# Turning q and k of the differential heads on VectorE instead of TensorE, and making the weights' parts for two row tiles at once

## The chip, the cores and the metric

The kernel runs on one core of a Trainium2 chip. Its time is the device time of one execution in microseconds (us). A core has these engines: PE (TensorE, the matrix unit; the loading of its stationary operand is shown as PEld), DVE (VectorE), ACT (ScalarE), POOL (GpSimd) and SP (SyncE, which here issues DMAs). Each works through a queue of its own, in order; semaphores hold an instruction until what it needs is there.

## The reference

Two layers, each on x of 256 rows (the sequence) and 2048 columns, all float32. A layer normalises x by rows (RMSNorm), multiplies by one wide weight `w_in` (2048 x 7168), and deals the columns out to three groups:

- a short gated convolution (768 columns wide): y_A = B * conv3(C * x_A) * silu(g_A);
- differential attention, 6 heads of 128 columns. q and k of a head are two halves of 64, each RMS-normalised by itself. The scores of each half go through a softmax with a distance bias, and the head's output is the first half's weighted v minus lambda times the second's, normalised and gated by silu(g_D);
- cross attention into 256 memory rows, 4 heads of 128; the memory has a projection of its own, `w_mem_kv`.

The three results side by side (2048 columns) are multiplied by `w_out` and added to x.

```
q = rmsnorm(d_q.reshape(b, s, 6, 2, 64), diff_q_norm_g[l])
k = rmsnorm(d_k.reshape(b, s, 6, 2, 64), diff_k_norm_g[l])
sc = einsum('bhcqd,bhckd->bhcqk', q, k) * 64**-0.5 + bias
o = softmax(sc) @ v ;  o[:, :, 0] - lam * o[:, :, 1]
```

## The kernel before, in words

**Three products for one.** Weights and the stationary side are split into a high part (rounded to the type float32r, on which PE runs fast) and a low part (the rest). A product is high x high + high x low + low x high: three matmuls, lines 237 to 239. A weight is streamed 128 rows (one *row tile*) x 512 columns at a time against two stationary tiles (the 256 rows of x are two tiles of 128), so one row tile of weights is used by six matmuls.

**Making the parts.** `load_w` (L204) loads two row tiles (a *pair*, 512 KB, CK = 2) by one DMA on SP's queue into `raw` (4 buffers), and then, for each row tile by itself, ACT writes `hi` (L218) and DVE writes `lo` = raw - hi (L219). For `w_mem_kv` a gain is multiplied in at the same time (L221, L222). `hi` and `lo` have 8 buffers each (PARTS), one for a row tile.

**Blocks.** `block` (L228) computes 512 output columns into two accumulators `acc` in PSUM: it goes through the 16 row tiles of the weight, a pair at a time. After each pair it takes one step of *side work* from a queue (`run_side`, L168): generators that transpose, split and score what earlier blocks left. `flush_side` empties the queue.

**The stages.** The memory's keys and values of both layers come first (4 blocks), then for each layer: six blocks for q, k, v and gate of the differential heads (L591, b = 0 to 5), two for the memory heads, six for the convolution, and four for the output projection (L690). The blocks b = 0, 1, 2 hold q and k: b = 0 has q of heads 0 to 3, b = 1 the rest of q and k of heads 0 and 1, b = 2 k of heads 2 to 5.

**q and k.** After each of these blocks `normed` (L296) takes the sums of squares by halves (ACT L302, DVE L303), an rsqrt by a chain of small DVE instructions (L159 to L163), and writes the scaled block `nat`, one 128x512 tile for each 128 rows (DVE L311). `qk_T` (L388) then turns it: for each of the two tiles, four 128x128 transposes on PE into a PSUM tile `ptq` (L394), and from there ACT and DVE write the split parts into `yT`: for q a high copy (ACT L402) and a low (DVE L403); for k two high copies with the gain (ACT L412, L413), a low (DVE L417) and a copy of it to the other 64 partitions (DVE L419). Both tiles are two steps of side work.

**Heads.** `diff_head` (L424) has the score matmuls L429 and L430, which read those parts, then bias, maximum, softmax (L434 to L447), transposes and the product with v (`weighted`, L356). They are put into the side queue after b = 5.

**Square turns.** `turn32` (L332) is there before the change for the gate of the convolution: DVE's transpose works on squares of 32x32, and 16 instructions, each for one pair of 32-partition groups, turn a whole 128x128 pattern; four of them are one step of side work.

**What sets the order.** The text of the program gives priorities; a scheduler that plans with estimated durations puts the instructions of each engine into their final order when the program is built, and buffers are handed out in that order. On the chip each engine keeps that order. So a change in one helper can move instructions of others.

Of the kernel before, what the change touches and what calls it, by code (L numbers as in the profile page):

```python
# [18 lines left out]
P = 128  # L19
D_MODEL = 2048  # L20
SEQ = 256
DEPTH = 2
NT = SEQ // P
# [4 lines left out]
CG = W_CONV // P  # L28
DH = W_DIFF // P
HALF = 64  # L30
MH = W_MEM // P
EPS = 1e-6
NB = 512
CK = 2
PARTS = 8
# [8 lines left out]
def encoder(ctx: ExitStack, tc: tile.TileContext, x, mem, norm_g, w_in, conv_w, conv_b,  # L44
            dq_g, dk_g, lq1, lk1, lq2, lk2, head_g, mem_norm_g, w_mem_kv, mq_g, mk_g, w_out, out):
    nc = tc.nc
# [8 lines left out]
    wp = pool("wp", 3)  # L55
    keep = pool("keep", 1)
    tmp = pool("tmp", 2)
# [3 lines left out]
    ps_t = pool("ps_t", 2, PSUM)  # L61
# [66 lines left out]
    kgain = const.tile([P, DEPTH], F32, name="kgain")  # L128
# [37 lines left out]
    side = deque()  # L166
# [21 lines left out]
    def in_order(*ins):  # L188

        if pinned[0]:  # L190
            for i in ins:
                tc.keep_in_program_order(i)
# [11 lines left out]
    def load_w(rows, cols, gains_of=None, step=CK, head=False):  # L204

        raw = wp.tile([P, CK, NB], F32, tag="raw", name=nm("raw"), bufs=4)
        at = 0
        for lo, n in cols:
            for j in range(0, CK, step):
                (nc.scalar if head and j == 0 else nc.sync).dma_start(  # L210
                    raw[:, j:j + step, at:at + n], rows[j * P:(j + step) * P, lo:lo + n].rearrange("(j p) c -> p j c", p=P))
            at += n
        parts = []
        for j in range(CK):
            hi = wp.tile([P, NB], F32R, tag="hi", name=nm("hi"), bufs=PARTS)
            lo_ = wp.tile([P, NB], F32R, tag="lo", name=nm("lo"), bufs=PARTS)
            if gains_of is None:
                nc.scalar.copy(hi, raw[:, j])  # L218
                nc.vector.tensor_tensor(lo_, raw[:, j], hi.bitcast(F32), ALU.subtract)  # L219
            else:  # L220
                ins = [nc.scalar.activation(hi, raw[:, j], AF.Copy, scale=gains_of(j)),  # L221
                       nc.vector.scalar_tensor_tensor(lo_, raw[:, j], gains_of(j), hi.bitcast(F32),  # L222
                                                      ALU.mult, ALU.subtract)]
                in_order(*ins)
            parts.append((hi, lo_))
        return parts

    def block(stat, w, cols, order, steps=1, gain=None, before=None, apart=0):  # L228

# [63 lines left out]
    def col(st, which, t):  # L293
        return st[:, which, t:t + 1]

    def normed(acc, gs, st):  # L296

        ng = NB // gs
        ss = small.tile([P, NT, ng], F32, tag=f"ss{ng}", name=nm("ss"))
        for t in range(NT):  # L300
            sq = tmp.tile([P, NB], F32, tag="nat", name=nm("sq"), bufs=4)
            nc.scalar.activation(sq, acc[t], AF.Square)  # L302
            nc.vector.tensor_reduce(ss[:, t], sq.rearrange("p (g d) -> p g d", d=gs), AX.X, ALU.add)  # L303
            nc.vector.tensor_scalar(ss[:, t], ss[:, t], col(st, R2_64 if gs == HALF else R2_128, t), EPS,
                                    ALU.mult, ALU.add)
        r = rsqrt(ss.rearrange("p t g -> p (t g)"), NT * ng).rearrange("p (t g) -> p t g", t=NT)
        res = []
        for t in range(NT):
            nc.vector.tensor_scalar(r[:, t], r[:, t], col(st, R, t), None, ALU.mult)
            y = tmp.tile([P, NB], F32, tag="nat", name=nm("nat"), bufs=4)  # L310
            nc.vector.tensor_tensor(y.rearrange("p (g d) -> p g d", d=gs),  # L311
                                    acc[t].rearrange("p (g d) -> p g d", d=gs),
                                    r[:, t].unsqueeze(2).to_broadcast([P, ng, gs]), ALU.mult)
            res.append(y)
        return res

    def turn(nat, dests):

# [13 lines left out]
    def turn32(dst, src):  # L332

        n = src.shape[-1] // P
        B = 32
        for b in range(P // B):
            for a in range(P // B):
                nc.vector.transpose(
                    dst[b * B:(b + 1) * B, 0:n].rearrange("p j (t a c) -> p t j a c", a=P // B, c=B)[:, :, :, a, :],
                    src[a * B:(a + 1) * B].rearrange("p t (j b c) -> p t j b c", b=P // B, c=B)[:, :, :, b, :])  # L340
            yield
# [43 lines left out]

    ROWS = (slice(0, HALF), slice(HALF, P))

    def qk_T(l, yT, k2, nat, q, k):  # L388

        for t in range(NT):  # L390
            ts = slice(t * P, (t + 1) * P)
            pt = ps_t.tile([P, 4, P], F32, tag="t", name=nm("ptq"))
            for j in range(4):
                nc.tensor.transpose(pt[:, j, :], nat[t][:, j * P:(j + 1) * P], ident)  # L394
            if q is not None:
                c0, h0, nh = q
                a = c0 // P
                for c in range(2):
                    own, other = ROWS[c], ROWS[1 - c]
                    src = pt[own, a:a + nh, :]  # L400
                    hi = yT[own, c, h0:h0 + nh, ts]
                    nc.scalar.copy(hi, src)  # L402
                    nc.vector.tensor_tensor(yT[other, c, h0:h0 + nh, ts], src, hi.bitcast(F32), ALU.subtract)  # L403
            if k is not None:
                c0, h0, nh = k
                a = c0 // P
                for c in range(2):
                    own, other = ROWS[c], ROWS[1 - c]
                    src = pt[own, a:a + nh, :]
                    g = kgain[own, l:l + 1]  # L410
                    hi = yT[own, c, CG + h0:CG + h0 + nh, ts]
                    nc.scalar.activation(hi, src, AF.Copy, scale=g)  # L412
                    nc.scalar.activation(yT[other, c, CG + h0:CG + h0 + nh, ts], src, AF.Copy, scale=g)  # L413
                    for at, n, dst, d0 in ((0, min(nh, 4 - h0), yT, CG + DH + h0), (4 - h0, h0 + nh - 4, k2, 0)):
                        if n > 0:
                            lo = dst[own, c, d0:d0 + n, ts]
                            nc.vector.scalar_tensor_tensor(lo, pt[own, a + at:a + at + n, :], g,  # L417
                                                           hi[:, at:at + n].bitcast(F32), ALU.mult, ALU.subtract)
                            nc.vector.tensor_copy(dst[other, c, d0:d0 + n, ts], lo)  # L419
            yield  # L420

    scored = set()

# [140 lines left out]
    for l in range(DEPTH):  # L564
# [10 lines left out]
        acc = block(memT, w_mem_kv[l], [(W_MEM, NB)], ALLK, gain=gm, before=mem_square if l == 0 else None)  # L575
# [7 lines left out]
    for l in range(DEPTH):  # L583
        st = stats_of(ssx, "st")


        yT = T_tile("yT")
        k2 = keep.tile([P, 2, DH - 4, SEQ], F32R, tag="bgT", name=nm("k2"))
        v = keep.tile([P, NT, W_DIFF], F32, tag="v", name=nm("v"))
        ga = keep.tile([P, NT, W_DIFF], F32, tag="ga", name=nm("ga"))  # L590
        for b in range(6):  # L591
            acc = block(xT, w_in[l], [(C_D + b * NB, NB)], ALLK)
            if b < 3:
                side.append(qk_T(l, yT, k2, normed(acc, HALF, st),
                                 (0, 0, 4) if b == 0 else (0, 4, 2) if b == 1 else None,
                                 (256, 0, 2) if b == 1 else (0, 2, 4) if b == 2 else None))
            else:
                for t in range(NT):
                    if b == 3:
                        nc.scalar.activation(v[:, t, 0:NB], acc[t], AF.Copy, scale=col(st, R, t))  # L600
                    elif b == 4:
                        nc.scalar.activation(v[:, t, NB:768], acc[t][:, 0:256], AF.Copy, scale=col(st, R, t))
                        silu2(ga[:, t, 0:256], acc[t][:, 256:512], st, t)
                    else:
                        silu2(ga[:, t, 256:768], acc[t], st, t)
# [66 lines left out]
        acc = block(xT, w_in[l], [(C_X + NB, 256), (C_C + NB, 256)], ALLK)  # L672
# [5 lines left out]
        acc = block(xT, w_in[l], [(C_C, NB)], ALLK)  # L678
# [57 lines left out]
```

## Time and profile before

| | |
|---|---|
| median of 3 runs | 960.23 us (959.88 to 960.38) |
| the profiled execution | 960.4 us, of which the span of the program's instructions is 958.6 us |
| PE busy | 99%, 4458 matmuls |
| DVE busy | 72%, 1560 instructions |
| ACT busy | 55%, 1091 instructions |
| granted clock of PE | 1.00 |
| DMA | 175.27 MB, mean 183 GB/s |

The page of the profile gives busy times by engine and by group of instructions (a line of the kernel, an engine, an operation, the tiles written and read). A group's row ends with its busy time, the mean ns of one instruction, and the idle time of the engine just before them with what ended it. Two instructions of one engine can overlap: a matmul lasts longer than the distance to the next. The waits list who waited for whom: total us, times, longest. The timeline lists instructions by start and duration; "x2" is a row of two that follow each other.

### The profile page before, as it was taken

To read this page: it belongs to the slowest core of one execution; us is meant where nothing else is said; L and a number is where in the kernel's file an instruction comes from. 1 tells how busy PE (TensorE), PEld (TensorE's weight loads), DVE (VectorE), ACT (ScalarE), POOL (GpSimd) and SP (SyncE) were. 2 spreads that over 40 slices of the span, in tenths; PEclk is the share of its full clock that TensorE was granted. 3 is DMA by queue.
4 is the path that set the end of the run, shared out by engine and by line. 5 is a ranking of instruction groups with operands and counts; after the bars stand their busy time and mean duration, and the time that the engine had idled before them with its cause. 6 is when DMAs were issued, how large, how long until landed. Compare 5 with 4: busy or idle time off the path is not lost.

```text
span 958.6 us, 13432 instructions
## 1 busy us (share of the span) xinstructions
PE 952.0 (99%) x4458; PEld 788.6 (82%) x4458; DVE 691.9 (72%) x1560; ACT 555.4 (58%) x1091; POOL 1.4 (0%) x8
## 2 busy tenths in 40 slices
PE   9999999999999999999999999999999999999998
PEld 6888888888888888888888888888888888888886
DVE  5767778865787888576766678856787788577663
ACT  5857756755656655554555556754666655554442
POOL 0000000000000000000000000000000000000000
PEclk9999999999999999999999999999999999999999
DMA  7775565576554554655555666566455555554661
GB/s 251 266 272 188 178 179 178 172 215 187 171 174 154 164 159 150 208 176 175 176 178 193 181 179 190 177 202 197 153 174 176 157 171 172 172 182 161 218 221 66
DMA packets 103530, 175.27 MB, mean 183 GB/s; under 512 B 6318, under 2 KB 29732, under 8 KB 103460
## 3 DMA queue, kind: packets, MB, share of 16 engines
q1 hardware_dynamic: 102116, 173.09, 57.3%
q10 hardware_dynamic: 1344, 1.33, 0.5%
q8 instruction: 35, 0.57, 0.2%
q14 instruction: 35, 0.29, 0.1%
HBM read 172.29 MB, written 2.10 MB: 182 GB/s over the span
## 4 chain that ended last, share of the span: by engine, by line
PE 94%; DMA 2%; DVE 2%; ACT 1%; issue 1%; ACTq 0%; DVEq 0%
PE acc L237 29%; PE acc L239 29%; PE acc L238 29%; DMA raw<-in_w_mem_kv_dram 2%; PE po L368 2%; DVE lo L222 1%; PE ptT L361 1%; ACT hi L221 1%; PE pt L506 1%; PE s L476 1%; PE s L430 1%; PE s L429 1%; PE ptq L394 1%; PE py L353 0%; PE pt L323 0%
## 5 line engine op out<-in xcount | busy, mean ns | idle before, releaser
L218 ACT CAST hi<-raw 128x512 fp32r<-128x512 f32 x576 | 355.2, 621 | 323.4 <-PE acc L239 199.2
L219 DVE TENSOR_TENSOR lo<-raw,hi 128x512 fp32r<-128x512 f32 x576 | 393.5, 690 | 181.8 <-ACT hi L218 175.6
L237 PE MATMUL acc<-hi,xT 128*128 128x512 f32 x896 | 353.1, 395 | 0.0
L238 PE MATMUL acc<-lo,xT 128*128 128x512 f32 x896 | 351.7, 392 | 0.0
L239 PE MATMUL acc<-hi,xT 128*128 128x512 f32 x896 | 350.1, 393 | 0.0
L237 PEld LDWEIGHTS acc<-hi,xT 128*128 128x128 f32 x896 | 168.4, 188 | 34.0
L238 PEld LDWEIGHTS acc<-lo,xT 128*128 128x128 f32 x896 | 168.4, 188 | 33.9
L239 PEld LDWEIGHTS acc<-hi,xT 128*128 128x128 f32 x896 | 167.9, 188 | 33.9
L239 PE MATMUL acc<-hi,yT 128*128 128x512 f32 x256 | 98.8, 392 | 0.0
L238 PE MATMUL acc<-lo,yT 128*128 128x512 f32 x256 | 98.6, 390 | 0.0
L237 PE MATMUL acc<-hi,yT 128*128 128x512 f32 x256 | 96.8, 393 | 0.0
L222 DVE SCALAR_TENSOR_TENSOR lo<-raw,cva,hi 128x512 fp32r<-128x512 f32 x64 | 46.1, 749 | 17.1 <-ACT hi L221 16.6
L238 PEld LDWEIGHTS acc<-lo,yT 128*128 128x128 f32 x256 | 48.1, 188 | 9.9
L239 PEld LDWEIGHTS acc<-hi,yT 128*128 128x128 f32 x256 | 47.9, 188 | 9.9
L237 PEld LDWEIGHTS acc<-hi,yT 128*128 128x128 f32 x256 | 47.8, 188 | 9.5
L221 ACT ACTIVATE hi<-raw,cva 128x512 fp32r<-128x512 f32 x64 | 43.7, 719 | 20.3 <-PE acc L239 13.1
L238 PE MATMUL acc<-lo,memT 128*128 128x512 f32 x124 | 48.6, 392 | 0.0
L239 PE MATMUL acc<-hi,memT 128*128 128x512 f32 x124 | 48.4, 390 | 0.0
L237 PE MATMUL acc<-hi,memT 128*128 128x512 f32 x124 | 44.5, 395 | 0.4 <-ACT mv L577 0.4
L238 PEld LDWEIGHTS acc<-lo,memT 128*128 128x128 f32 x124 | 23.3, 188 | 4.9
L239 PEld LDWEIGHTS acc<-hi,memT 128*128 128x128 f32 x124 | 23.3, 188 | 4.8
L237 PEld LDWEIGHTS acc<-hi,memT 128*128 128x128 f32 x124 | 22.8, 188 | 5.3 <-ACT mv L577 0.8
(152 smaller groups left out, 700.7 us busy)
## 6 DMA issues: line engine op xcount, KB each, us to landing
raw<-in_w_in_dram SPq DMA_DIRECT2D x192, 512.0 KB
raw<-in_w_out_dram SPq DMA_DIRECT2D x64, 512.0 KB
raw<-in_w_in_dram SPq DMA_DIRECT2D x64, 256.0 KB
raw<-in_w_mem_kv_dram SPq DMA_DIRECT2D x31, 512.0 KB
xs<-in_x_dram SPq DMA_DIRECT2D x8, 256.0 KB
xs<-in_mem_dram SPq DMA_DIRECT2D x7, 256.0 KB
out_dram<-xs SPq DMA_DIRECT2D x8, 128.0 KB
out_dram<-xs ACTq DMA_DIRECT2D x8, 128.0 KB
```

The costliest lines, as they stand in the source:

```text
L218: nc.scalar.copy(hi, raw[:, j])
L219: nc.vector.tensor_tensor(lo_, raw[:, j], hi.bitcast(F32), ALU.subtract)
L221: ins = [nc.scalar.activation(hi, raw[:, j], AF.Copy, scale=gains_of(j)), nc.vector.scalar_tensor_tensor(lo_, raw[:, j], gains_of(j), hi.b ...
L222: nc.vector.scalar_tensor_tensor(lo_, raw[:, j], gains_of(j), hi.bitcast(F32), ALU.mult, ALU.subtract)]
L237: nc.tensor.matmul(acc[t], sh, hi, start=first, stop=False)
L238: nc.tensor.matmul(acc[t], sh, lo, start=False, stop=False)
L239: nc.tensor.matmul(acc[t], sl, hi, start=False, stop=last)
L361: nc.tensor.transpose(pt[:, k, i * P:(i + 1) * P], e[:, i, k * P:(k + 1) * P], ident)
L368: nc.tensor.matmul(po[:, i, :], eT[:, k, i * P:(i + 1) * P], v[:, k, h * P:(h + 1) * P], start=k == 0, stop=k == NT - 1)
L394: nc.tensor.transpose(pt[:, j, :], nat[t][:, j * P:(j + 1) * P], ident)
L429: nc.tensor.matmul(s[c][:, i, :], qi, k_first(yT, c, h), start=True, stop=False)
L430: nc.tensor.matmul(s[c][:, i, :], qi, k_second(yT, k2, c, h), start=False, stop=True)
```

## The change

1. `load_w`: `hi` and `lo` become tiles for the pair, 128 x 2 x 512, with four buffers each in place of eight (the same memory). Without a gain one ACT instruction and one DVE instruction make both row tiles (1024 elements a partition); with a gain there is still one for each row tile.
2. `qk_T`: the four PE transposes of each tile and the PSUM tile go. `normed(..., whole=True)` writes both tiles of `nat` into one tile `both` (of the tag `e`, which the heads' scores use too), `turn32` turns it into the SBUF tile `whole` by 16 DVE instructions of 32 x 256 elements, and the parts are written from there for all 256 rows at once: half as many instructions, twice as long. `whole` borrows the memory of a later tile (`mqT`, `mga` or `bgx`).
3. The copy of k's low part to the other partitions goes from DVE (L419) to ACT.
4. The steps of side work are cut anew: four for the turn, then one for each half of q and of k.

```diff
-            hi = wp.tile([P, NB], F32R, tag="hi", name=nm("hi"), bufs=PARTS)
-            lo_ = wp.tile([P, NB], F32R, tag="lo", name=nm("lo"), bufs=PARTS)
-            if gains_of is None:
-                nc.scalar.copy(hi, raw[:, j])
-                nc.vector.tensor_tensor(lo_, raw[:, j], hi.bitcast(F32), ALU.subtract)
+        hi = wp.tile([P, CK, NB], F32R, tag="hi", name=nm("hi"), bufs=PARTS // CK)
+        lo_ = wp.tile([P, CK, NB], F32R, tag="lo", name=nm("lo"), bufs=PARTS // CK)
+        if gains_of is None:
+            nc.scalar.copy(hi, raw)
+            nc.vector.tensor_tensor(lo_, raw, hi.bitcast(F32), ALU.subtract)
...
+        both = tmp.tile([P, NT, NB], F32, tag="e", name=nm("nat")) if whole else None
...
-            pt = ps_t.tile([P, 4, P], F32, tag="t", name=nm("ptq"))
-            for j in range(4):
-                nc.tensor.transpose(pt[:, j, :], nat[t][:, j * P:(j + 1) * P], ident)
...
+        whole = keep.tile([P, NB // P, SEQ], F32, tag=tag, name=nm("qk"))
+        yield from turn32(whole, nat)
+        if q is not None:
+            c0, h0, nh = q
+            a = c0 // P
+            for c in range(2):
+                own, other = ROWS[c], ROWS[1 - c]
+                src = whole[own, a:a + nh, :]
+                hi = yT[own, c, h0:h0 + nh, :]
+                nc.scalar.copy(hi, src)
+                nc.vector.tensor_tensor(yT[other, c, h0:h0 + nh, :], src, hi.bitcast(F32), ALU.subtract)
+                yield
+        if k is not None:
...
+                nc.scalar.activation(hi, src, AF.Copy, scale=g)
+                nc.scalar.activation(yT[other, c, CG + h0:CG + h0 + nh, :], src, AF.Copy, scale=g)
...
+                        nc.vector.scalar_tensor_tensor(lo, whole[own, a + at:a + at + n, :], g,
+                                                       hi[:, at:at + n].bitcast(F32), ALU.mult, ALU.subtract)
+                        nc.scalar.copy(dst[other, c, d0:d0 + n, :], lo)
+                yield
```

In the changed program the lines are some three or four lower: `hi` is L216 and `lo` L217 (L220 and L221 with a gain), the matmuls L234 to L236, the square sums L299 and L300, `nat` L309, the transposes L336, the parts of q and k L397, L398, L408, L409, L413 and L415, the scores L425 and L426, the bias L430.

More of the change, by code (lines that the diff above doesn't have):

```diff
@@ L294, in col, with normed @@
         return st[:, which, t:t + 1]
-    def normed(acc, gs, st):
+    def normed(acc, gs, st, whole=False):
         ng = NB // gs
@@ L307, in normed @@
         res = []
+        both = tmp.tile([P, NT, NB], F32, tag="e", name=nm("nat")) if whole else None
         for t in range(NT):
             nc.vector.tensor_scalar(r[:, t], r[:, t], col(st, R, t), None, ALU.mult)
-            y = tmp.tile([P, NB], F32, tag="nat", name=nm("nat"), bufs=4)
+            y = both[:, t] if whole else tmp.tile([P, NB], F32, tag="nat", name=nm("nat"), bufs=4)
             nc.vector.tensor_tensor(y.rearrange("p (g d) -> p g d", d=gs),
@@ L314, in normed @@
             res.append(y)
-        return res
+        return both if whole else res
     def turn(nat, dests):
@@ L386, in encoder @@
     ROWS = (slice(0, HALF), slice(HALF, P))
-    def qk_T(l, yT, k2, nat, q, k):
-        for t in range(NT):
-            ts = slice(t * P, (t + 1) * P)
-            pt = ps_t.tile([P, 4, P], F32, tag="t", name=nm("ptq"))
-            for j in range(4):
[L394 to L420, printed above, removed]
@@ new lines, in qk_T @@
+    def qk_T(l, yT, k2, nat, q, k, tag):
+        whole = keep.tile([P, NB // P, SEQ], F32, tag=tag, name=nm("qk"))
[11 more added lines that the diff above has]
+        if k is not None:
+            c0, h0, nh = k
+            a = c0 // P
+            for c in range(2):
+                own, other = ROWS[c], ROWS[1 - c]
+                src = whole[own, a:a + nh, :]
+                g = kgain[own, l:l + 1]
+                hi = yT[own, c, CG + h0:CG + h0 + nh, :]
+                nc.scalar.activation(hi, src, AF.Copy, scale=g)
+                nc.scalar.activation(yT[other, c, CG + h0:CG + h0 + nh, :], src, AF.Copy, scale=g)
+                for at, n, dst, d0 in ((0, min(nh, 4 - h0), yT, CG + DH + h0), (4 - h0, h0 + nh - 4, k2, 0)):
+                    if n > 0:
+                        lo = dst[own, c, d0:d0 + n, :]
+                        nc.vector.scalar_tensor_tensor(lo, whole[own, a + at:a + at + n, :], g,
+                                                       hi[:, at:at + n].bitcast(F32), ALU.mult, ALU.subtract)
+                        nc.scalar.copy(dst[other, c, d0:d0 + n, :], lo)
+                yield
@@ L593, in encoder @@
             if b < 3:
-                side.append(qk_T(l, yT, k2, normed(acc, HALF, st),
+                side.append(qk_T(l, yT, k2, normed(acc, HALF, st, whole=True),
                                  (0, 0, 4) if b == 0 else (0, 4, 2) if b == 1 else None,
-                                 (256, 0, 2) if b == 1 else (0, 2, 4) if b == 2 else None))
+                                 (256, 0, 2) if b == 1 else (0, 2, 4) if b == 2 else None,
+                                 ("mqT", "mga", "bgx")[b]))
             else:
```

15 lines of the change are left out of this document (6 added, 9 removed).

## The prediction

> **What bounds the kernel now.** I read the page first (busy shares, then the chain), then the waits, then the timeline.
>
> ```profile
> span 958.6 us, 13432 instructions
> PE 952.0 (99%) x4458; PEld 788.6 (82%) x4458; DVE 691.9 (72%) x1560; ACT 555.4 (58%) x1091; POOL 1.4 (0%) x8
> PE 94%; DMA 2%; DVE 2%; ACT 1%; issue 1%; ACTq 0%; DVEq 0%
> ```
> ```profile
> ACT hi L218 <- PE acc L239: 199.2, 267, 1.9
> DVE lo L219 <- ACT hi L218: 175.6, 287, 1.8
> ```
> PE is 99% busy and 94% of the chain. Neither wait is PE's: ACT waits until PE gives a weight buffer back, and DVE waits for ACT. The makers of `hi` and `lo` run ahead as far as their buffers let them. So only two things move the end: PE work removed, and moments at which PE runs out of prepared operands.
>
> How far ahead? These rows give the rhythm where little else runs:
>
> ```profile
> 198.99 0.39 PE L239 MATMUL acc<-hi,xT 128*128 128x512 f32 x1
> ...
> 199.42 0.62 ACT L218 CAST hi<-raw 128x512 fp32r<-128x512 f32 x1 [0.73 <-PE acc L239]
> 200.78 0.62 ACT L218 CAST hi<-raw 128x512 fp32r<-128x512 f32 x1 [0.74 <-DVE lo L219]
> ```
> PE uses up one row tile (six matmuls) in 1.36 us, a pair in 2.72, and a matmul in 0.227. A freed buffer is refilled 0.43 us after its last matmul started, 0.2 after PE has moved on. Durations for the rest:
>
> ```profile
> L219 DVE TENSOR_TENSOR lo<-raw,hi 128x512 fp32r<-128x512 f32 x576 | 393.5, 690 | 181.8 <-ACT hi L218 175.6
> L218 ACT CAST hi<-raw 128x512 fp32r<-128x512 f32 x576 | 355.2, 621 | 323.4 <-PE acc L239 199.2 <-DVE lo L219 93.7 <-DMA raw<-in_w_in_dram 7.6
> L338 DVE STREAM_TRANSPOSE bgT<-bg 32x256 f32<-32x256 f32 x32 | 13.9, 436 | 0.4
> L311 DVE TENSOR_TENSOR nat<-acc,rsy 128x512 f32<-128x512 f32 x20 | 12.8, 683 | 0.1
> L303 DVE TENSOR_REDUCE ss<-sq 128x8 f32<-128x512 f32 x12 | 8.0, 683 | 0.0
> L412 ACT ACTIVATE yT<-ptq,kgain 64x512 fp32r<-64x512 f32 x8 | 5.5, 684 | 2.1 <-PE ptq L394 1.9
> L403 DVE TENSOR_TENSOR yT<-ptq,yT 64x512 fp32r<-64x512 f32 x8 | 5.3, 686 | 1.0 <-ACT yT L402 0.8
> L654 DVE TENSOR_TENSOR yT<-z,yT 128x256 fp32r<-128x256 f32 x12 | 5.0, 416 | 0.0
> L653 ACT CAST yT<-z 128x256 fp32r<-128x256 f32 x12 | 4.8, 403 | 2.2 <-DVE z L652 2.2
> L402 ACT CAST yT<-ptq 64x512 fp32r<-64x512 f32 x8 | 4.5, 581 | 1.4 <-PE ptq L394 0.9 <-DVE yT L403 0.4
> ```
> ```profile
> 154.07 0.17 DVE L162 TENSOR_TENSOR rsa<-rsa,ss 128x16 f32<-128x16 f32 x1
> 154.27 0.17 DVE L163 SCALAR_TENSOR_TENSOR rsy<-rsa,rsy 128x16 f32<-128x16 f32 x1
> ...
> 354.69 0.15 DVE L163 SCALAR_TENSOR_TENSOR rsy<-rsa,rsy 128x2 f32<-128x2 f32 x1
> 354.76 0.68 DVE L219 TENSOR_TENSOR lo<-raw,hi 128x512 fp32r<-128x512 f32 x1
> 355.37 0.15 DVE L161 SCALAR_TENSOR_TENSOR rsa<-rsy 128x2 f32<-128x2 f32 x1
> ...
> 370.58 1.77 DVE L338 STREAM_TRANSPOSE bgT<-bg 32x256 f32<-32x256 f32 x4
> ```
> Start to start, a queued `lo` occupies DVE 0.61 us, not 0.69; a step of the rsqrt chain 0.20; but a transpose 0.45 (four in 1.77), longer than it lasts.
>
> **The change, part by part.**
>
> *PE transposes removed.* Six blocks (three a layer) lose eight each.
>
> ```profile
> 142.12 0.39 PE L237 MATMUL acc<-hi,xT 128*128 128x512 f32 x1
> 142.35 1.04 PE L394 MATMUL ptq<-ident,nat 128*128 128x128 f32 x8
> 143.15 0.48 PE L238 MATMUL acc<-lo,xT 128*128 128x512 f32 x1
> 143.46 0.39 PE L239 MATMUL acc<-hi,xT 128*128 128x512 f32 x1
> ```
> L239 would start two steps of 0.227 after L237; it starts 1.34 after, so a group costs 0.89. 6 x 0.89 = **5.3 us gained**, the whole possible gain.
>
> *Pairs.* From 256 to 512 elements DVE grows by 274 ns and ACT by 218, so I take 1.24 us for a `lo` of 1024 (occupying 1.15) and 1.06 for a `hi`. Nearest bounds: 690 and 621 (one half), 1380 and 1242 (two halves). DVE and ACT save time, but PE's 99% hides all of it. What counts is that a buffer comes back only when both row tiles are done: from release to need there are three pairs, 8.16 us; less 0.2, 1.06 and 1.24 that leaves **5.7 us spare**. Before it was 7 x 1.36 - 0.2 - 0.62 - 0.69 = 8.0.
>
> *Square transposes added.* 6 x 16 on DVE. In the order of the changed program all 16 of a block stand in one run with no `lo` between: 16 x 0.45 = **7.2 us, more than 5.7**. Load of such a block on DVE: eight `lo` 9.2, run 7.2, two square sums and two products of `nat` at 0.6 each 2.4, rsqrt chain about 2.8, two lows of q or k about 2.4: 24.0, while PE needs 8 x 2.72 = 21.8. So each block also hands a debt on.
>
> The Trainium skill, "VectorE: DVE Perf Modes", section "Two Vector instructions with no wait between them", says that an instruction whose input or output starts in another group of 32 partitions than the last one's waits until all earlier ones have finished. That is so for each of the 16; the rows above agree (0.45 apart where each lasts 0.436, against a `lo` that is followed 0.08 early). Without it the run would last 16 x 0.36 = 5.8 us, and the sum below would be rival 3's. Its section "Rules for kernel authors" advises TensorE for a full 128x128 transpose if PSUM will do; here, per block, 0.89 us on PE stands against 7.2 on DVE.
>
> *Scores pulled ahead.* With qk's steps changed, the built order puts the score matmuls of the first three differential heads into the blocks after k's, between matmuls of `acc`, where before they came later. PE keeps its order, so a score that waits for qk's copies holds all matmuls behind it:
>
> ```
> L234 Matmult acc<-hi x2                (a pair's first two)
> L425 Matmult s<-yT [waits Activation]  (ACT's copy of k, after the run)
> L235 Matmult acc<-lo ...
> ```
> ACT's copies start when the run ends: L397, L408, L409, from SBUF now, 0.62 + 0.72 + 0.72 = 2.1 us (the 64x512 rows plus 0.035, by which 128x256 L653 exceeds its PSUM twin; bounds 0.58 and 0.69 each).
>
> *The ledger.* Clock zero is PE leaving the block of the first q; pair n starts at 2.72n plus earlier waits, its `hi` 0.2 after pair n-4 is left.
> - Layer 0, run 1: DVE does `lo` 7 until 14.0, run until 21.3, `lo` 8 ready 22.6; PE has its first two matmuls done at 22.2: 0.4. Run 2: statistics put `lo` 16 at 38.2, run 39.4 to 46.6, copies 48.7; PE reaches the score at 47.15: 1.55. Run 3: 66.7 to 73.9, `lo` 75.1 against 75.0: 0.1. Then ACT must do four 64x1024 copies (1.1 each), a softmax (2.0), three `hi` and L415's copies of k's lows, which went from DVE to ACT; the third head's score has its last copy at 85.2 and PE is there at 83.9: 1.3. **3.4.**
> - Layer 1: the order differs. Run 1 ends at 17.9; ACT's copy of q stands ahead of the next `hi`, ready 20.0 against 19.5: 0.5. Run 2, 35.9 to 43.1: scores ready 45.2 against 44.5 and 49.25 against 48.05: 1.9. Run 3, 62.9 to 70.1: `lo` 71.3 against 70.1: 1.2; third head 81.4 against 79.6: 1.8. **5.4.**
>
> *The seam into the output projection.*
>
> ```profile
> 453.94 0.46 PE acc L239 x2
> 454.40 0.47 PE acc L237 x2
> ```
> Two output blocks alternate here while the conv columns of y come late, and PE has no gap. In pairs, three of four buffers wait for conv, and the next block's first `hi` goes into the buffer that PE leaves just before it needs it: 0.2 + 1.06, less two transposes (0.2), about 1.1, and 0.2 on the next `lo`. Two layers: **2.6 us.**
>
> *At nothing.* ACT's q and k copies and SP's queue: its order is the same but for one weight load of the last projection that moves behind two stores.
>
> ```profile
> 900.47 1.62 SPq L700 DMA_DIRECT2D out_dram<-xs  x2
> ```
> 1.6 us, for a pair that is seven pairs (19 us) away; if that cover were gone it would cost 1.6. The tiles that qk borrows (`mqT`, `mga`, `bgx`, `e`) were last read, and are next written, a block or more away; the two `e` are freed by the runs, as the ledger has them.
>
> **The sum.** Profiled execution 960.4 us: span 958.6 and 1.8 around it; the median of three runs is 960.23, 0.17 lower. -5.3 + 3.4 + 5.4 + 2.6 = +6.1: 966.5, against the median **966.3 us**, 0.6% slower.
>
> **The rivals.**
> 1. *Faster: the spare covers the run.* If DVE enters each run with its debt paid, four pairs carry PE over it, and if the scores find their copies done, only the 5.3 us remain: 955 (957.5 with the seams). For it: before, 14 such transposes ran nearly in one piece without a gap on PE. Against: there the spare was 8.0, and PE had other work between. It decides where run plus debt falls below 5.7.
> 2. *Deeper: the halves cost more than one slope.* With a `lo` at its bound of 1.38 each block hands on 1.1 us more; nine waits at 0.5 to 1 more, and like gaps at the heads' transposes, add 6 to 15: 972 to 981. For it: DVE is at 19.6 of 22.6 us in one of these blocks already:
> ```profile
> 163.00:185.60 22.60, 22.60 (x105) 18.83 (x104) 19.64 (x48) 15.76 (x30) 0.00 (x0) 1.00 0.59 175
> ```
> (DVE is the third busy column.) Against: both slopes come from two sizes of the same operation.
> 3. *Same: shorter runs.* At 0.36 a transpose, or with less debt than I count, each wait is up to 1.4 shorter, 8.8 shrinks to about 0.6, and -5.3 + 0.6 + 2.6 gives 958 to 962. At 0.36 the transposes would follow each other 0.08 early, as the `lo` above do. For it: only the one row of four shows their spacing. Against: that row, and the gaps of 0.01 between them in its 1.77.
>
> **Chances.** A measurement of this kernel can tell about 0.2% (1.9 us) from no change. Forecast (962.2 to 972) 0.50; rival 1 0.22; rival 2 0.13; rival 3 0.15. So faster 0.22, same 0.15, slower 0.63. Cases of both signs are in play: the likeliest one's own range is 962 to 972; the range for 8 in 10 is 954.5 to 975, which takes in the gain without any wait and the lower part of rival 2.
>
> **What would show it.** Right: PE has gaps that were not there: in the stretch of the q and k blocks of each layer, right after the six runs of 16 L336, with ACT L408/L409 or `lo` named as what ended them; one gap of about 1.1 us at each seam, ended by ACT `hi` L216. A run lasts 7.2 us; `lo` 1.24 and `hi` 1.06. Wrong: no such gaps (rival 1), or a run near 5.8 (rival 3), or gaps at other lines, in the head stage or the first 60 us, which I take as unchanged.

## The result and the profile after

| | before | after |
|---|---|---|
| median | 960.23 us (959.35 to 960.56, 9 runs) | **963.08 us** (962.56 to 963.66, 9 runs) |
| ratio | | 1.0031, 95% interval 1.0021 to 1.0041 |
| the profiled execution | span 958.6 us | span 960.9 us |

The change makes the kernel 0.3% slower: +2.85 us, less than half of the +6.1 that the sum gave. The page of the changed kernel first (the span; busy time by engine; the chain; then three groups with busy time, mean ns, idle time before):

```profile
span 960.9 us, 12463 instructions
PE 948.6 (99%) x4410; PEld 782.7 (81%) x4410; DVE 690.7 (72%) x1324; ACT 508.3 (53%) x791; POOL 1.4 (0%) x8
PE 85%; DVE 10%; issue 2%; ACT 1%; DMA 1%; SPq 0%; DVEq 0%
L217 DVE TENSOR_TENSOR lo<-raw,hi 128x1024 fp32r<-128x1024 f32 x288 | 351.0, 1222 | 174.3 <-ACT hi L216 172.8
L216 ACT CAST hi<-raw 128x1024 fp32r<-128x1024 f32 x288 | 302.5, 1051 | 309.6 <-PE acc L236 269.2
L336 DVE STREAM_TRANSPOSE qk<-nat 32x256 f32<-32x256 f32 x96 | 41.8, 436 | 1.3
```

PE has 48 instructions fewer and 3.4 us less to do, and yet the span is longer: PE's time is lost in gaps. (ACT's 53% stands against 58% on the page of before; the 55% in the table of before is too low.) DVE's share of the chain went from 2% to 10%: over several stretches it is now DVE that the end waits for. The waits name the gaps (waiter, what it waited for, total us, times, longest; PEld is the load of PE's stationary operand, listed beside the matmul that it is for):

```profile
PEld acc L235 <- DVE lo L217: 3.9, 5, 2.0
PEld acc L234 <- ACT hi L216: 1.9, 2, 0.9
PEld pt L642 <- issue: 1.8, 2, 0.9
```

Five waits for `lo`, two for `hi`, two ahead of a transpose of the convolution: nine gaps, of which the waits of before have none. No row of the changed kernel's waits has a score (`s`, L425 or L426) that waits for a copy of q or k.

**After the turns.** The timeline around the five runs of 16 that a gap follows, with two of the runs themselves:

```profile
141.04 7.19 DVE L336 STREAM_TRANSPOSE qk<-nat 32x256 f32<-32x256 f32 x16
...
148.78 0.61 PE L234 MATMUL acc<-hi,xT 128*128 128x512 f32 x2
149.54 0.50 PE L235 MATMUL acc<-lo,xT 128*128 128x512 f32 x1 [0.15 <-DVE lo L217]
149.88 0.39 PE L236 MATMUL acc<-hi,xT 128*128 128x512 f32 x1
...
174.16 0.28 PE L425 MATMUL s<-yT 128*128 128x256 f32 x1
174.83 0.50 PE L235 MATMUL acc<-lo,xT 128*128 128x512 f32 x1 [0.40 <-DVE lo L217]
...
201.16 0.28 PE L426 MATMUL s<-yT 128*128 128x256 f32 x1
201.56 0.50 PE L235 MATMUL acc<-lo,xT 128*128 128x512 f32 x1
...
598.25 0.28 PE L425 MATMUL s<-yT 128*128 128x256 f32 x1
598.53 0.50 PE L235 MATMUL acc<-lo,xT 128*128 128x512 f32 x1
...
615.75 7.19 DVE L336 STREAM_TRANSPOSE qk<-nat 32x256 f32<-32x256 f32 x16
622.17 0.28 PE L426 MATMUL s<-yT 128*128 128x256 f32 x1
622.97 1.22 DVE L217 TENSOR_TENSOR lo<-raw,hi 128x1024 fp32r<-128x1024 f32 x1
624.25 0.50 PE L235 MATMUL acc<-lo,xT 128*128 128x512 f32 x1 [1.80 <-DVE lo L217]
```

How a gap is read: the two L234 at 148.78 would be followed at 149.23 (two steps of 0.227); L235 starts at 149.54, 0.31 late, and its successor another 0.11 late: 0.42. A score matmul is followed after 0.12. In the same way, and with 0.11 of the successor each, the others are 0.67, 0.40, 0.27 and 2.07; after the first run of layer 1 there is none. Together **3.8 us**. Each ends when the first `lo` behind the run is ready; at 622.97 that `lo` starts 0.03 after the run's end, and PE has stood since 622.29.

**At the seams** into the output projection (layer 0; layer 1 repeats it):

```profile
450.86 1.23 DVE L217 TENSOR_TENSOR lo<-raw,hi 128x1024 fp32r<-128x1024 f32 x1 [1.52 <-ACT hi L216]
...
452.46 0.41 DVE L198 TENSOR_TENSOR yT<-py,yT 128x256 fp32r<-128x256 f32 x1
453.02 0.41 PE L642 MATMUL pt<-ident,ux 128*128 128x128 f32 x2 [0.49 <-DVE yT L198]
453.93 1.05 ACT L216 CAST hi<-raw 128x1024 fp32r<-128x1024 f32 x1 [2.65 <-PE acc L236]
455.03 0.96 PE L234 MATMUL acc<-hi,yT 128*128 128x512 f32 x3 [0.69 <-ACT hi L216]
```

Two gaps. The one expected: `hi` starts at 453.93, when PE has left the pair whose buffer it takes, and L234 waits for it until 455.03 (0.93 late, with 0.2 ahead of it and 0.11 behind). And one not expected: L642 needs a PSUM bank that DVE's L198 still has to read; L198 stood behind a `lo` of 1.23 us, and PE lost 0.65. In all 1.9 us a layer, **3.8 us**.

**In the first block of layer 0**, where x is still being turned and split, small gaps that before did not have:

```profile
104.97 1.05 ACT L216 CAST hi<-raw 128x1024 fp32r<-128x1024 f32 x1
...
105.68 0.61 PE L236 MATMUL acc<-hi,xT 128*128 128x512 f32 x2
105.92 0.83 ACT L200 ACTIVATE xT<-pt,cvb 128x256 fp32r<-128x256 f32 x2
106.05 1.23 DVE L217 TENSOR_TENSOR lo<-raw,hi 128x1024 fp32r<-128x1024 f32 x1 [0.55 <-ACT hi L216]
106.44 0.50 PE L234 MATMUL acc<-hi,xT 128*128 128x512 f32 x1
106.78 0.40 PE L235 MATMUL acc<-lo,xT 128*128 128x512 f32 x1
...
107.19 0.87 DVE L201 SCALAR_TENSOR_TENSOR xT<-pt,cvb,xT 128x256 fp32r<-128x256 f32 x2
107.24 0.40 PE L235 MATMUL acc<-lo,xT 128*128 128x512 f32 x1
107.77 0.63 PE L502 MATMUL pt<-ident,xs 128*128 128x128 f32 x4
```

L200 of ACT and L201 of DVE are short, but each stands behind an instruction for a whole pair: 0.31 + 0.11 at 106.44 and 0.30 at 107.77, **0.7 us**.

**The ledger closes.** -5.3 (PE transposes) + 3.8 + 3.8 + 0.7 = +3.0; PE also reached the first block of layer 0 0.8 us earlier than in the profile of before. That part differs by up to 1.0 from one profiled execution to the next (the first accumulating matmul starts between 6.16 and 7.19 us in the profiles of this study), so it isn't put to the change. Left is +2.2; the spans of the two profiled executions differ by 2.3. The medians differ by 2.85, and single executions of the changed kernel by up to 1.1.

### The profile page after: what moved, and what is told of

It is laid out like the page before. It is cut to its first block, busy times and chain, and to the rows that moved or that the text cites. A ratio compares the mean times of both kernels' runs of the same rounds, so it can differ in the third digit from the quotient of the medians.

```text
span 960.9 us, 12463 instructions
## 1 busy us (share of the span) xinstructions
PE 948.6 (99%) x4410; PEld 782.7 (81%) x4410; DVE 690.7 (72%) x1324; ACT 508.3 (53%) x791; POOL 1.4 (0%) x8
## 4 chain that ended last, share of the span: by engine, by line
PE 85%; DVE 10%; issue 2%; ACT 1%; DMA 1%; SPq 0%; DVEq 0%
PE acc L236 26%; PE acc L234 26%; PE acc L235 26%; DVE lo L217 4%; DVE qk L336 3%; PE po L366 2%; PE pt L502 1%; PE ptT L359 1%; ACT hi L216 1%; DMA xs<-in_mem_dram 1%; PE s L472 1%; DVE ss L300 1%; PE py L351 0%; PE s L426 0%; PE s L425 0%
## 5 line engine op out<-in xcount | busy, mean ns | idle before, releaser
L217 DVE TENSOR_TENSOR lo<-raw,hi 128x1024 fp32r<-128x1024 f32 x288 | 351.0, 1222 | 174.3 <-ACT hi L216 172.8
L216 ACT CAST hi<-raw 128x1024 fp32r<-128x1024 f32 x288 | 302.5, 1051 | 309.6 <-PE acc L236 269.2
L235 PE MATMUL acc<-lo,xT 128*128 128x512 f32 x896 | 352.4, 393 | 2.5 <-DVE lo L217 2.3
L236 PE MATMUL acc<-hi,xT 128*128 128x512 f32 x896 | 349.4, 392 | 0.0
L234 PE MATMUL acc<-hi,xT 128*128 128x512 f32 x896 | 345.5, 394 | 0.1
L235 PEld LDWEIGHTS acc<-lo,xT 128*128 128x128 f32 x896 | 168.4, 188 | 37.7 <-DVE lo L217 3.9
L234 PEld LDWEIGHTS acc<-hi,xT 128*128 128x128 f32 x896 | 168.2, 188 | 34.7 <-ACT xT L200 0.6
L236 PEld LDWEIGHTS acc<-hi,xT 128*128 128x128 f32 x896 | 167.9, 188 | 33.6
L234 PE MATMUL acc<-hi,yT 128*128 128x512 f32 x256 | 99.0, 393 | 1.4 <-ACT hi L216 1.4
L235 PE MATMUL acc<-lo,yT 128*128 128x512 f32 x256 | 99.5, 391 | 0.0
L236 PE MATMUL acc<-hi,yT 128*128 128x512 f32 x256 | 98.8, 392 | 0.0
L234 PEld LDWEIGHTS acc<-hi,yT 128*128 128x128 f32 x256 | 47.9, 188 | 11.9 <-ACT hi L216 1.9
L221 DVE SCALAR_TENSOR_TENSOR lo<-raw,cva,hi 128x512 fp32r<-128x512 f32 x64 | 45.6, 748 | 16.6 <-ACT hi L220 16.4
L235 PEld LDWEIGHTS acc<-lo,yT 128*128 128x128 f32 x256 | 48.1, 188 | 9.8
L236 PEld LDWEIGHTS acc<-hi,yT 128*128 128x128 f32 x256 | 47.8, 188 | 9.5
L220 ACT ACTIVATE hi<-raw,cva 128x512 fp32r<-128x512 f32 x64 | 42.7, 717 | 19.8 <-PE acc L236 13.1
L236 PE MATMUL acc<-hi,memT 128*128 128x512 f32 x124 | 48.6, 392 | 0.0
L235 PE MATMUL acc<-lo,memT 128*128 128x512 f32 x124 | 48.4, 390 | 0.0
L234 PE MATMUL acc<-hi,memT 128*128 128x512 f32 x124 | 44.4, 395 | 0.1
L336 DVE STREAM_TRANSPOSE qk<-nat 32x256 f32<-32x256 f32 x96 | 41.8, 436 | 1.3
L235 PEld LDWEIGHTS acc<-lo,memT 128*128 128x128 f32 x124 | 23.3, 188 | 5.0
L236 PEld LDWEIGHTS acc<-hi,memT 128*128 128x128 f32 x124 | 23.3, 188 | 4.8
```

The lines of the kernel that those rows point to most:

```text
L216: nc.scalar.copy(hi, raw)
L217: nc.vector.tensor_tensor(lo_, raw, hi.bitcast(F32), ALU.subtract)
L220: in_order(nc.scalar.activation(hi[:, j], raw[:, j], AF.Copy, scale=gains_of(j)), nc.vector.scalar_tensor_tensor(lo_[:, j], raw[:, j], gai ...
L221: nc.vector.scalar_tensor_tensor(lo_[:, j], raw[:, j], gains_of(j), hi[:, j].bitcast(F32), ALU.mult, ALU.subtract))
L234: nc.tensor.matmul(acc[t], sh, hi, start=first, stop=False)
L235: nc.tensor.matmul(acc[t], sh, lo, start=False, stop=False)
```

## The experiments

The **theory** after the result: PE waits for `lo` and nothing else after the turns, because a run holds DVE for 7.2 us while DVE can be only 5.7 us ahead; the seams and the first block come from the pairs alone. **Rivals**: DVE's load in these blocks makes the gaps, however it is cut; the seams come from the moved order; and the step on record, that scores wait for the copies of q and k. All kernels were timed in five rounds beside the kernel before; gaps are read from the timelines as above.

| kernel | median us | ratio to before (95%) | gaps after turns | seams | first block |
|---|---|---|---|---|---|
| the change | 963.08 | 1.0031 (1.0021 to 1.0041) | 3.8 | 3.8 | 0.7 |
| e1_rows | 956.40 | 0.9965 (0.9952 to 0.9979) | 1.0 | 0 | 0 |
| e2_pairs | 963.98 | 1.0041 (1.0028 to 1.0054) | no turn on DVE | 3.8 | 0.7 |
| e7_spread | 961.88 | 1.0017 (1.0009 to 1.0026) | 2.6 | 3.8 | 0.7 |
| e8_rows_spread | **954.84** | 0.9944 (0.9932 to 0.9957) | 0 | 0 | 0 |
| e9_scores_after | 963.78 | 1.0039 (1.0027 to 1.0051) | 4.9 | 3.8 | 0.7 |
| e3_late | 963.27 | 1.0033 (1.0020 to 1.0045) | 3.5 | 3.8 | 0.7 |
| e4_five | 964.42 | 1.0046 (1.0031 to 1.0061) | 5.6 | 1.0 | 0 |
| e4c_cuts (its control) | 972.34 | 1.0127 (1.0114 to 1.0140) | 9.2 | 3.8 | 0 |
| e10_five | 959.51 | 0.9995 (0.9985 to 1.0005) | 0 | 1.0 | 0 |
| e10c_cuts (its control) | 962.64 | 1.0035 (1.0021 to 1.0049) | 3.9 | 3.8 | 0 |

**One part without the other: e1_rows and e2_pairs.** e1_rows is the changed kernel with the loop of before in `load_w`:

```diff
-        hi = wp.tile([P, CK, NB], F32R, tag="hi", name=nm("hi"), bufs=PARTS // CK)
-        lo_ = wp.tile([P, CK, NB], F32R, tag="lo", name=nm("lo"), bufs=PARTS // CK)
...
+        for j in range(CK):
+            hi = wp.tile([P, NB], F32R, tag="hi", name=nm("hi"), bufs=PARTS)
+            lo_ = wp.tile([P, NB], F32R, tag="lo", name=nm("lo"), bufs=PARTS)
...
```

> Only the turn on DVE; the weights' parts are made row tile by row tile again, with eight buffers each, as in the kernel before. Theory (a pair's buffer comes back too late): PE's gaps at the seams (1.9 us a layer in the changed kernel), the 0.6 at the heads of the first block and nearly all of the 3.8 us after the turns go, because a freed row tile is refilled at once and the spare is 8.0 us against a run of 7.2; the 5.3 us of PE transposes stay gained: 956.5 us (955 to 958). Rival 1 (DVE's load makes the gaps, not the buffers): the seams go, but the 3.8 us after the turns stay or grow, since eight pairs of row tiles occupy DVE 0.6 us more a block than eight pairs made at once: about 959.5. Rival 2 (the seams come from the moved order of the blocks): the seams stay: about 960.

e2_pairs is the kernel before with the same edit the other way round.

> Only the pairs; q and k are turned on PE as in the kernel before. Theory (pairs alone make the seams): 1.9 us at each seam and 0.6 in the first block of layer 0, 0.8 less at the very start, no gap in the q and k blocks: 960.2 + 3.8 + 0.6 - 0.8 = 963.8 us, as slow as the whole change or slower. Rival (the seams come from the order that the new steps of q and k give): 960 us or less, with no gap at the seams.

956.40 and 963.98 us against 960.19 for before in the same call: the two parts of the change are worth -3.8 and +3.8. Alone, the turn on DVE is a gain, and the pairs, which save DVE and ACT time, are a loss. The waits of e1_rows, then of e2_pairs:

```profile
PEld acc L238 <- DVE lo L219: 1.2, 3, 0.6
```
```profile
PEld acc L234 <- ACT hi L216: 1.9, 2, 0.9
PEld pt L642 <- issue: 1.8, 2, 0.9
```

With row tiles nothing is left of the seams, and of the waits for `lo` 1.0 us in layer 0 (0.26 and 0.71), though its runs are the same 7.19 to 7.20 us. With pairs and no turn, the seams and the first block stand exactly as in the changed kernel, and no wait for `lo` is there. So rival 2 of the experiment falls, and rival 1 in its plain form too: sixteen `lo` at 0.61 load DVE more than eight at 1.15, and the gaps shrank. The parts do not add up: -3.8 + 3.8 is 0, both together +2.85. The 2.85 match the 2.8 us of waits for `lo` that the runs cost when the buffers come in pairs and do not cost when they come one by one (3.8 - 1.0); the two single effects are known to about 1.3 us each, so this is an agreement and no proof.

**The length of the hold: e7_spread and e8_rows_spread.** The turn of a block waits until the eighth pair of the next block and then goes four transposes at a time, each group and the `lo` ahead of it held in their written order:

```diff
+                one = nc.vector.transpose(
...
+                if apart:
+                    tc.keep_in_program_order(one)
+            if apart:
+                last[0] = one.ins
...
+            with tc.issue_after(last[0]) if last[0] is not None else nullcontext():
+                return load_w(...)
```

> The changed kernel with its 16 transposes of a block held in four groups of four, with one lo of a pair ahead of each group; pairs kept. Theory (one hold of 7.2 us outlasts the spare of 5.7): a hold is now 1.8 us, the gaps after the turns go (3.8 to under 0.8), the seams stay at 1.9 each: 959.6 us (959 to 960.5). Rival (the debt counts: DVE has 24.0 us to do in such a block against PE's 21.8, however it is cut): gaps of 2.5 us or more stay in the q and k blocks, 962 us or more.

> Both: parts row tile by row tile, and the transposes in four groups of four with lo between. Theory (buffers and length of the hold): no gap of either kind is left, 955 to 956 us, at most 1 us below the kernel with row tiles and runs of 16. Rival (DVE's load): like that kernel or slower, 958 or more, with gaps after the turns.

e7_spread: 961.88, 1.2 us better than the change, with 2.6 us of gaps left where the theory allowed 0.8. Here the theory was wrong and the rival right (gaps of 2.5 or more; the time is 0.1 below the 962 that it gave): with pairs, cutting the hold is not enough. The edit also starts the turns later, so the grouping and the place are not told apart in this run. The windows of e7_spread from the end of the third q/k block of layer 1 up to the gap (columns: stretch, its length, then busy time of PE, PEld, DVE, ACT):

```profile
599.40:634.90 35.50, 35.19 (x162) 28.99 (x160) 34.49 (x65) 24.05 (x35) 0.00 (x0) 1.00 0.53 164
```

DVE is busy for 34.49 of 35.50 us: it does not catch up, and the gap comes at the end of this stretch (PE's L235 at 635.24 waits for `lo`), although no run of transposes in it is longer than 1.8 us and DVE is never longer than 4.4 us without a `lo` (602.49 to 606.89). e8_rows_spread does the same with row tiles, at the same late place, and has no gap at all:

```profile
139.45 1.77 DVE L349 STREAM_TRANSPOSE qk<-nat 32x256 f32<-32x256 f32 x4
141.25 1.29 DVE L219 TENSOR_TENSOR lo<-raw,hi 128x512 fp32r<-128x512 f32 x2
142.58 1.78 DVE L349 STREAM_TRANSPOSE qk<-nat 32x256 f32<-32x256 f32 x4
```

It is the fastest of the study, **954.84 us**, 5.35 below before: the whole of the 5.3 us that the transposes on PE had cost, and 8.2 below the change. It is also 1.6 below e1_rows, where 1 at most was expected: the 1.0 us of gaps that e1_rows shows is gone, and the rest is within the spread of its runs (955.45 to 957.92). Hold, debt and spare all count; the theory in its short form, hold against spare, was too simple.

**How far DVE may be ahead: e4_five, e10_five and their controls.** Five pairs of `hi` and `lo` need 8 KB more a partition. e4_five takes it from `raw` (three buffers) and `nat` (three), e10_five from `nat` (two) and `eT` (one), and both from three small tiles; each control makes the same cuts with four pairs.

```diff
-PARTS = 8
+PARTS = 10
```

> The changed kernel with five pairs of hi and lo in place of four (spare 8.4 us instead of 5.7, the parts still made by pairs); to make room raw has three buffers, nat three and three small tiles two, as in the control e4c_cuts. Theory (what counts is how far DVE can be ahead, not that two row tiles are one instruction): the gaps after the turns fall from 3.8 to under 1.2 us and those at the seams from 3.8 to under 1, so 4 to 6 us less than the control, 957 to 959.5. Rival (DVE's backlog alone, 24.0 us of work against 21.8 of PE, a spare cannot help): not over 1.5 us less than the control.

> Control for e4_five: the changed kernel with the same smaller buffers of raw, nat and three small tiles, and four pairs as before. If the cuts cost nothing: 963.1 us, with the gaps of the changed kernel (3.8 after the turns, 3.8 at the seams). If the third load in flight was needed: more, with gaps ended by the DMA of raw.

> The changed kernel with five pairs of hi and lo in place of four, and raw at its four buffers; the room comes from nat (two buffers) and eT (one), as in the control e10c_cuts. Theory (what counts is how far DVE can be ahead: spare 8.4 us against 5.7): the gaps after the turns fall from 3.8 to under 1 us and the seams from 1.9 to about 0.5 each, as they did with five pairs and three raw: 957 us (956 to 958.5), 5 to 7 below the control. Rival (the pair itself, one instruction for two row tiles, makes the gaps): within 2 us of the control.

> Control: the changed kernel with two buffers of nat and one of eT, four pairs. If these cuts cost nothing, 963.1 us with the gaps of the changed kernel (3.8 after the turns, 3.8 at the seams); if they cost, the new gaps lie in the heads and the gates, not after the turns.

The fifth pair gained 7.9 us over its control in the first case and 3.1 in the second. e4_five is no clean case: its median stayed above the change, with ACT waiting 65 us for loads (10 in the change) and a gap of 3.4 that no `lo` ended (PE waited for an accumulator that DVE's L309 had still to read). In e10_five no gap is left after the turns, with runs of 16 and pairs unchanged, and 0.5 at each seam: the rival, that one instruction for two row tiles is itself the cause, falls. (The planner also moved the early scores out of layer 1 there, so not every tenth is the spare's.) The forecast of 957 was missed by 2.5, and a part of that is seen: one gap of 3.0 us in the memory stage.

```profile
57.91 0.50 PE L235 MATMUL acc<-hi,memT 128*128 128x512 f32 x1 [2.83 <-ACT mv L574]
```

A part of the rest goes with the clock: the five of its eleven runs with a granted clock of 0.999 or 1.0 took 957.8 to 958.7 us, the six with 0.996 to 0.998 took 959.5 to 961.9. The stretches of half clock described at the end would do that, but only the run with 957.93 us (clock 1.0) has a trace, so this is not shown. e4c_cuts was not the harmless control that it was meant to be: with three `raw`, 9.3 us slower than the change. Gaps ended by the loads had been expected for that case; but those in its q and k blocks are ended by `lo`, as its waits show:

```profile
PEld acc L235 <- DVE lo L217: 8.9, 4, 3.0
```

A load's buffer comes free when `lo` has been made from it, so by the program a run that holds DVE also holds up the loads; how much of the 9.3 us that makes was not separated.

**The step on record: e9_scores_after and e3_late.** e9_scores_after keeps the first three heads' scores behind the block that they are written after:

```diff
-                nc.tensor.matmul(s[c][:, i, :], qi, k_first(yT, c, h), start=True, stop=False)
+                one = nc.tensor.matmul(s[c][:, i, :], qi, k_first(yT, c, h), start=True, stop=False)
+                if h < 3 and c == 0 and i == 0:
+                    tc.keep_in_program_order(one)
```

> The changed kernel with the score matmuls of the first three heads held behind the block after which they are written (as they stood before), so none is between the q and k blocks' matmuls. As recorded in the prediction (scores wait for the copies): 6.6 us of waits would go, 956.5. Theory from the profile after (they never waited, since each half's copies start in the middle of a run; they only load DVE with two biases of 0.6 us and a maximum ahead of or behind the third run, and give PE 0.94 us a head of work that needs no weights): the gap after the third run of layer 1 goes from 2.1 to 1.0 to 1.8, all others stay, 962 to 963.

Not a microsecond of the 6.6 was there to be had: 963.78, 0.7 above the change (1.1 when each is taken against before in its own call). The new theory was right about that and wrong about the sign elsewhere: the gap after the third run of layer 1 fell from 2.07 to 0.99, but that after the third of layer 0 rose from 0.40 to 2.16. In e9_scores_after:

```profile
199.92 0.61 PE L234 MATMUL acc<-hi,xT 128*128 128x512 f32 x2
202.42 0.50 PE L235 MATMUL acc<-lo,xT 128*128 128x512 f32 x1 [1.89 <-DVE lo L217]
```

The early scores had been cover: PE work that lets DVE catch up.

e3_late exchanges the loops of the q/k turn, so that no half of q or k is complete before the run ends:

```diff
-        for b in range(P // B):
-            for a in range(P // B):
+        for x in range(P // B):
+            for y in range(P // B):
+                a, b = (x, y) if late else (y, x)
```

> The changed kernel with the two loops of the q and k turn exchanged, so that each half of q and k is complete only when all 16 transposes are done (in the changed kernel the first half is complete after eight); same instructions, and the built order puts the first of the early scores a quarter of a block later. The step on record took the copies to start at the end of a run, and PE to wait 6.6 us for them: if copies that start at the end hold PE, 965 to 967. Theory (PE waits for lo, never for these copies): 962.5 to 964, all gaps in the q and k blocks still ended by lo.

963.27, as the theory had it: 3.5 us of gaps, all ended by `lo`. It shows that late copies need not cost; it does not show what they would cost with the scores where the change has them, because the planner put the first score a quarter of a block later. That was not tried. One profile has such a wait all the same. In e4c_cuts, where PE reaches the first early score of layer 0 sooner after the run's first half, ACT's copy L409 ends at 176.46 and the score starts at 176.51, 0.25 us late (this is in the 9.2 of the table):

```profile
PEld s L425 <- ACT yT L409: 0.5, 1, 0.5
```

So the wait that the prediction feared can occur, 0.25 us of it here, where the copies also start in mid-run; no other profile of the study lists one.

## Why the prediction was right in sign and wrong in size

| step | forecast | measured |
|---|---|---|
| PE transposes removed | -5.3 | -5.3: e8_rows_spread, which has no gaps, is 5.35 below before |
| `lo` and `hi` of a pair | 1.24, 1.06 | 1.22, 1.05 |
| a run of 16 | 7.2 | 7.19 to 7.20 |
| waits after the turns, for `lo` or `hi` | 2.2 (0.4, 0.1, 0.5, 1.2) | 3.8 |
| waits after the turns, for scores | 6.6 (1.55, 1.3, 1.9, 1.8) | 0 |
| seams | 2.6 | 3.8 |
| first block of layer 0 | not named | 0.7 |

**The step that failed is "Scores pulled ahead"**, in the sentence that ACT's copies start when the run ends. Three quarters of the 8.8 us rested on it. Without it the prediction's own terms give -5.3 + 2.2 + 2.6 = -0.5, no change; the measured sign agrees with the forecast only because the waits for `lo`, the seams and the first block cost 3.5 us more than forecast. That the time also fell into the likeliest range (962.2 to 972) was luck of the same kind. The timeline of the changed kernel around the second run of layer 0 and, below, the third head's scores:

```profile
166.33 7.19 DVE L336 STREAM_TRANSPOSE qk<-nat 32x256 f32<-32x256 f32 x16
...
169.93 0.62 ACT L397 CAST yT<-qk 64x512 fp32r<-64x512 f32 x1 [0.41 <-DVE qk L336]
170.45 0.72 ACT L408 ACTIVATE yT<-qk,kgain 64x512 fp32r<-64x512 f32 x1
171.20 0.72 ACT L409 ACTIVATE yT<-qk,kgain 64x512 fp32r<-64x512 f32 x1
...
208.05 0.62 ACT L415 CAST yT<-yT 64x512 fp32r<-64x512 f32 x1
...
209.77 0.62 ACT L415 CAST k<-k 64x512 fp32r<-64x512 f32 x1
209.86 0.28 PE L425 MATMUL s<-yT 128*128 128x256 f32 x1
```

A run fills `whole` by groups of 32 partitions, so its first eight transposes complete partitions 0 to 63, the first half of every head, and the copies of that half need no more: 166.33 + 8 x 0.45 = 169.93, which is when L397 starts, in the middle of the run. The three copies are done at 171.92; the one score pulled ahead there, of the first half, stands at 174.16, which is where the ledger had PE (127.0 + 47.15), and finds them done. The third head was counted to the last of L415's four copies, which is `k` (of the last two heads) and starts at 209.77; what that head reads was done at 208.67, before PE was there. The error in both was to read "the copies read the turned tile" and "the scores read the copies" as waits for the whole, where the semaphore is on the part that is read.

**The ledger of DVE itself held.** With PE leaving the block of the first q at 127.0, the first run was put at 14.0 to 21.3 (measured 141.04 - 127.0 = 14.0, to 21.2) and its gap at 0.4 (0.42). Later gaps came out larger than forecast for `lo`. The ledger had put waits for scores ahead of them, in which DVE would have caught up; without those PE is at the next `lo` earlier. That is argued from the ledger; no run put such a wait back. e9_scores_after shows the same from the other side: a score matmul is PE work that needs no weights, 0.12 us each. Sixteen of them, 1.9 us, stand ahead of the `lo` behind the third run of layer 0 in the change, and without them the gap there is 1.8 longer.

**The seam** was right in place and mechanism and short by its second gap: 0.9 plus 0.3 around it for `hi` against 1.3, and 0.65 for L642, which the ledger did not follow through DVE's queue. That, and the 0.7 of the first block, are one thing that was missing: an instruction twice as long delays everything short behind it by up to its length, on ACT and DVE alike. "At nothing" was right for the copies themselves, for SP and for the borrowed tiles.

**The rivals.** The first (the spare covers the run, 955 to 957.5) is nearly what happens when the spare is 8.0: e1_rows, 956.40, with 1.0 us of gaps left. The second did not occur: `lo` took 1.22, not 1.38. The third did not either: the transposes follow each other 0.45 apart, as the run of 14 in the profile of before (6.27 us from 370.58) could already have told. The rule cited for it, from the Trainium skill, "VectorE: DVE Perf Modes", section "Two Vector instructions with no wait between them", agrees with all six runs (7.19 to 7.20 us); no run here has transposes that stay in one group of partitions, so the rule as the reason is not tested. The advice of its section "Rules for kernel authors", TensorE for a 128x128 transpose where PSUM will do, does not hold for this kernel, where PE is 99% busy: with parts made by row tiles, the turn on DVE is worth 3.8 us as written and 5.35 with the transposes in fours.

## What to carry to other kernels

Merging two instructions into one saves time on their engine and makes two things coarser: a buffer comes back only when all of it is done with, and short work behind the instruction waits for all of it; on an engine that is not the bound the saving is worth nothing, and the coarseness cost 3.8 us here. Before a long run of work is put on an engine that feeds the bound, compare three figures: how long it holds that engine, how far the engine can be ahead, and whether it catches up before the next run; and follow each consumer's wait to the part of the tile that it reads. A change of two parts is tried part by part: here one gained what the other lost.

## What the hardware showed besides

After some of the longer stops PE ran at half its clock. In e4_five (windows: the stretch, its length, PE busy, and after POOL's column the granted clock):

```profile
193.31:196.72 3.41, 0.43 (x4) 0.22 (x2) 3.34 (x9) 2.93 (x4) 0.00 (x0) 1.00 0.47 115
196.72:200.13 3.41, 3.19 (x8) 2.54 (x9) 3.37 (x7) 1.37 (x2) 0.00 (x0) 0.50 0.82 242
626.80:630.22 3.42, 1.44 (x6) 0.88 (x6) 3.35 (x7) 3.37 (x5) 0.00 (x0) 1.00 0.00 0
630.22:633.63 3.41, 3.41 (x9) 2.65 (x8) 3.35 (x6) 3.34 (x5) 0.00 (x0) 0.50 0.72 166
```

PE stood for 3.4 us, and its matmuls then came 0.43 us apart instead of 0.227 until 200.13, which lost another 1.4 us. The length of the stop alone does not decide: a stop of 2.1 us in the same execution (627.53 to 629.67) was followed by a half clock from 630.22 to 633.63, while the 2.0 us from 622.29 in the changed kernel and 3.0 us from 54.9 in e10_five were not.

The traces fit a rule of fixed windows. Both stretches of half clock last 3.41 us, their starts are 433.50 us apart, which is 127 times 3.413, and in each of the twelve profiles all changes of the granted clock lie on one grid of that step. Along these grids, the three windows in which PE was least busy (0.43 and 1.44 us in e4_five, 1.44 from 177.40 in e4c_cuts) are the three that a half clock follows; the next two (1.74 from 622.57 in the changed kernel, 1.77 from 627.96 in e4c_cuts) are followed by the full clock. So the 3.0 us of e10_five cost nothing more, as they fell on two windows (2.08 and 1.92 us busy). Three stretches are few, and no run moved a stop across such a border.
